# A new order for VectorE's and ScalarE's instructions up to the first FFN tiles

## The chip, the cores and the metric

The kernel runs on one core of one Trainium2 chip, as one launch. The metric is the device time of that launch in microseconds (us), as the median of several runs. A core has five engines that run at the same time, each through its own list of instructions in a fixed order: TensorE (PE, matrix products), VectorE (DVE), ScalarE (ACT), GpSimd (POOL) and SyncE (SP, which here only starts transfers). An engine whose next instruction needs something that is not ready stands still, with all that is behind it in its list. Products land in PSUM, a small memory in eight banks; everything else lies in SBUF.

## The reference, cut to what matters

One layer of a streaming encoder: an SSD (Mamba-2) branch and a latent attention (MLA) branch side by side, then a gated feed-forward network (FFN). There are 512 new tokens of one stream and 64 of another, which has a past.

```python
h = rmsnorm(x, p['norm_mix']);  proj = h @ p['w_in']          # z, xbc, dt, cq, ckv
xbc, conv_new = causal_conv(xbc, conv_buf, p['conv_w'], p['conv_b'])   # 4 taps, then silu
dt = softplus(dt_raw + p['dt_bias']);  A = -exp(p['a_log'])
y, h_new = ssd_scan(xh, dt, A, Bm, Cm, ssm_h0)                # chunked state space scan
y = (y + p['d_skip'][:, None] * xh) * silu(z);  y_ssd = rmsnorm(y, p['ssd_norm'])
q = rmsnorm(cq, p['q_norm']) @ p['w_uq']                      # q_nope, q_rope
q_rope = apply_rope(q[..., QK_NOPE:], cos, sin)
c_kv = rmsnorm(ckv_raw[..., :KV_LORA], p['kv_norm']);  k_rope = apply_rope(...)
o_lat = mla_attend(q_lat, q_rope, ...)                        # softmax over past and new keys
x = x + concatenate([y_ssd, o]) @ p['w_out']
hf = rmsnorm(x, p['norm_ffn'])
x = x + (silu(hf @ p['w_gate']) * (hf @ p['w_up'])) @ p['w_down']
```

The width is 1024, the FFN's 2816, with 8 SSD heads and 8 attention heads of 64. Everything is float32.

## The kernel before

All 576 tokens lie in the free dimension, in two halves of 288. Channels lie in the 128 partitions. A float32 product is made of three products of a rounded type: each operand is split into a high part and the rest (`wh` and `wl` of a weight), and high·high, high·rest and rest·high are added up in PSUM. The split of a weight tile of 128x1024 is a cast on ACT and a subtraction on DVE:

```python
112        act.copy(hi, raw)
113        dve.tensor_tensor(lo, raw, hi.bitcast(F32), ALU.subtract)
```

So each weight tile asks for one transfer (L119), 1.05 us of ACT and 1.22 us of DVE before PE can use it. Raw tiles and both parts share a few buffers in turn (`wpool`), so a split can also have to wait until PE has read an older weight.

The stages up to 280 us, with the lines that matter here:

- First projections and norms, up to about 45 us. L309 scales the compressed query `cq` by its norm, L313 the compressed key `ckv`. `sp_a`, `dt` and `dA` (L346 to L356) are the step sizes of the scan, small instructions on 128x40.
- Input tiles with the convolution, about 40 to 86 us. Eight tiles `ps_in` in the order 3, 6, 0, 2, 4, 1, 5, 7, two PSUM buffers in turn. DVE evicts each with three instructions (L382, L383, L384) into `up`; then ACT makes the first tap (L389), DVE three more (L391, `cacc`), ACT the tanh (L393), and DVE L395 and L396 write the result into `xsd` (tiles 0 to 3) or `bc` (4 to 7). PE can begin a tile when the tile two before it has been evicted.
- Rotary queries. PE makes `ps_qr0` and `ps_qr1` from `cqn` (made by L142 on ACT and L146 on DVE from `cq`), in the same two PSUM buffers. DVE multiplies with cosine and sine: L421 twice reads `ps_qr0` into `rrp`, L422 twice reads `ps_qr1` into `qt`, L423 twice combines them. Then the pool of these two PSUM buffers is closed, and new pools take its space: the first z tile `ps_z0` lies where `ps_qr0` was and so waits until both L421 have read that. POOL copies the rotated queries to their place (L601), and after them applies the causal mask to `cumb` (L500), on which the scan's exponentials `E` on ACT wait (L506).
- Gates `z` and the scan, 88 to 150 us. Halves of `ps_z` are evicted by L453 into `zh`, one of two banks each; ACT makes the tanh (L456) and DVE the gate (L457). For each chunk of tokens DVE makes `xdt` (L485), `xw` (L509), `E` times the products (L514), reads the outputs `ps_y` (L532, L539, L540), multiplies with the gate (L567) and carries the state `h` (L554, L555).
- Attention and the output projection, mixed, 120 to 260 us. `ps_q` and `ps_k` are evicted by L607 and L611, scores `sc` get a maximum (L640, DVE), the exponential with its sum (L641, ACT), and a scaling by the reciprocal (L642, L647); transposes and the products with the values follow (L679 to L704). The output projection's halves `ps_o` are added to the residual `x` by L735.
- FFN tiles from about 222 us to the end.

The order in which the engines go through all this is not the order in which the code makes the instructions. After the whole program is written, a table `ISSUE` names, for each engine, the numbers of its instructions in the order in which they are to be issued, and each is tied to the one before:

```python
1303        for a, b in zip(order, order[1:]):
1304            tc.add_manual_dep(made[b], made[a].name, info, reason="issue order")
```

The numbers count an engine's instructions as they were made; a range such as `67-68` stands for all in it. What an instruction waits for is worked out afterwards from the data and the buffers.

## Time and profile before

| | |
|---|---|
| time, median of 3 runs | 641.3 us (641.02 to 641.71) |
| the profiled execution | 639.76 us, span 638.1 us |
| TensorE | busy 627.0 us, 98% of the span, 4635 matmuls |
| weight load of TensorE | 598.9 us, 94% |
| VectorE | 543.5 us, 85%, 945 instructions |
| ScalarE | 400.9 us, 63%, 768 instructions |
| GpSimd | 110.4 us, 17% |
| TensorE's granted clock, mean | 0.998 of full speed |
| chain that ended last | TensorE 84%, VectorE 3%, ScalarE 1%, transfers 1% |

A row of the timeline gives the start, the time, the engine, the line of the code, the operation, what it writes and reads, the tile's shape, and a count, if several alike stand in a row; in brackets stands how long the engine was idle just before and what ended that. Instructions of one engine overlap a little, so that one row may begin some hundredths of a microsecond before the end of the last. Names come without their numbers in the profile: `ps_in` is any of the eight input tiles.

### The profile page before, as it was taken

To read this page: it belongs to the slowest core of one execution; us is meant where nothing else is said; L and a number is where in the kernel's file an instruction comes from. 1 tells how busy PE (TensorE), PEld (TensorE's weight loads), DVE (VectorE), ACT (ScalarE), POOL (GpSimd) and SP (SyncE) were. 2 spreads that over 40 slices of the span, in tenths; PEclk is the share of its full clock that TensorE was granted. 3 is DMA by queue.
4 is the path that set the end of the run, shared out by engine and by line. 5 is a ranking of instruction groups with operands and counts; after the bars stand their busy time and mean duration, and the time that the engine had idled before them with its cause. 6 is when DMAs were issued, how large, how long until landed. Compare 5 with 4: busy or idle time off the path is not lost.

```text
span 638.1 us, 12090 instructions
## 1 busy us (share of the span) xinstructions
PE 627.0 (98%) x4635; PEld 598.9 (94%) x4635; DVE 543.5 (85%) x945; ACT 400.9 (63%) x768; POOL 110.4 (17%) x164
## 2 busy tenths in 40 slices
PE   9999999999999999999999999999999999999996
PEld 8899999986787799999999999999999999999995
DVE  6999986899876699999999888988899789986555
ACT  7645436778775567766566676566757665767364
POOL 1322103101010000001300330033103220323323
PEclk9999999999999999999999999999999999999999
DMA  9322366322231133235643986398737892589914
GB/s 320 130 61 71 97 158 159 108 80 60 87 123 61 56 111 102 89 116 183 239 141 101 205 185 153 82 186 194 169 100 156 197 206 100 101 211 258 259 27 148
DMA packets 39593, 89.19 MB, mean 140 GB/s; under 512 B 4570, under 2 KB 14312, under 8 KB 39280
## 3 DMA queue, kind: packets, MB, share of 16 engines
q1 hardware_dynamic: 26416, 63.12, 30.5%
q0 software_dynamic: 12400, 24.73, 20.9%
q8 instruction: 36, 0.59, 0.4%
q10 hardware_dynamic: 720, 0.57, 0.3%
q14 instruction: 21, 0.17, 0.1%
HBM read 62.74 MB, written 24.53 MB: 137 GB/s over the span
## 4 chain that ended last, share of the span: by engine, by line
PE 84%; DVE 3%; ACT 1%; issue 1%; POOL 1%; DMA 1%; POOLq 0%; DVEq 0%; ACTq 0%
PE ps_x L852 21%; PE ps_d L1050 14%; PE ps_z L852 11%; PE ps_o L443 8%; PE ps_y L852 5%; PE ps_in L128 4%; PE ps_z L443 3%; PE ps_l L988 3%; PE ps_d L988 2%; PE ps_p L852 2%; PE sc L657 2%; PE pv L704 2%; PE ptp L679 1%; PE ps_v L590 1%; PE ps_q L443 1%
## 5 line engine op out<-in xcount | busy, mean ns | idle before, releaser
L852 PE MATMUL ps_x<-xop,wh_gu_S 128*128 128x288 f32 x504 | 101.7, 295 | 0.0
L852 PEld LDWEIGHTS ps_x<-xop,wh_gu_S 128*128 128x128 f32 x504 | 80.7, 188 | 0.2
L852 PE MATMUL ps_x<-xop,wl_gu_S 128*128 128x288 f32 x252 | 74.0, 294 | 0.0
L113 DVE TENSOR_TENSOR wl_gu_S<-gu,wh_gu_S 128x1024 fp32r<-128x1024 f32 x44 | 53.4, 1221 | 10.3 <-ACT wh_gu_S L112 6.8
L1064 POOL DMA_DIRECT2D acc<-fz x32 | 27.9, 907 | 167.2 <-ACT fz L1061 138.3
L112 ACT CAST wh_gu_S<-gu 128x1024 fp32r<-128x1024 f32 x44 | 46.3, 1052 | 15.9 <-PE ps_y L852 8.2
L852 PEld LDWEIGHTS ps_x<-xop,wl_gu_S 128*128 128x128 f32 x252 | 47.3, 188 | 0.0
L128 PE MATMUL ps_in<-xs,wh_in 128*128 128x288 f32 x256 | 45.3, 298 | 0.8 <-DVE sp_a L351 0.6
L128 PEld LDWEIGHTS ps_in<-xs,wh_in 128*128 128x128 f32 x256 | 37.6, 189 | 1.9 <-issue 0.9
L852 PE MATMUL ps_z<-xop,gu_a 128*128 128x288 f32 x252 | 38.3, 295 | 0.0
L852 PEld LDWEIGHTS ps_z<-xop,gu_a 128*128 128x128 f32 x252 | 35.0, 188 | 0.0
L852 PE MATMUL ps_z<-xop,wh_gu_S 128*128 128x288 f32 x168 | 34.9, 297 | 0.0
L852 PE MATMUL ps_x<-xop,wh_gu_A 128*128 128x288 f32 x168 | 34.6, 297 | 0.0
L852 PE MATMUL ps_y<-xop,wh_gu_A 128*128 128x288 f32 x168 | 33.9, 294 | 0.0
L112 ACT CAST wh_gu_A<-gu 128x1024 fp32r<-128x1024 f32 x22 | 23.1, 1051 | 10.4 <-PE ps_x L852 7.0
L443 PE MATMUL ps_o<-cat_y,wh_out 128*128 128x288 f32 x128 | 29.3, 312 | 0.4 <-ACT cat_y L142 0.4
L113 DVE TENSOR_TENSOR wl_gu_A<-gu,wh_gu_A 128x1024 fp32r<-128x1024 f32 x22 | 26.8, 1220 | 1.4 <-ACT wh_gu_A L112 1.0
L852 PEld LDWEIGHTS ps_z<-xop,wh_gu_S 128*128 128x128 f32 x168 | 27.2, 189 | 0.3 <-ACT wh_gu_S L112 0.3
L128 PE MATMUL ps_in<-xs,wl_in 128*128 128x288 f32 x128 | 27.4, 296 | 0.0
L852 PEld LDWEIGHTS ps_x<-xop,wh_gu_A 128*128 128x128 f32 x168 | 27.2, 189 | 0.1
L852 PEld LDWEIGHTS ps_y<-xop,wh_gu_A 128*128 128x128 f32 x168 | 26.9, 188 | 0.0
L443 PE MATMUL ps_z<-xs,wh_z 128*128 128x288 f32 x128 | 26.4, 299 | 0.0
(384 smaller groups left out, 2012.0 us busy)
## 6 DMA issues: line engine op xcount, KB each, us to landing
gu<-in_w_gu SPq DMA_DIRECT2D x44, 512.0 KB, 5.3
wr_d<-in_w_down SPq DMA_DIRECT2D x18, 512.0 KB, 4.1
acc<-fz POOLq DMA_DIRECT2D x16, 288.0 KB, 6.6
acc<-da POOLq DMA_DIRECT2D x16, 288.0 KB, 7.8
acc<-dc POOLq DMA_DIRECT2D x16, 288.0 KB, 8.4
wr_in<-in_w_in SPq DMA_DIRECT2D x8, 512.0 KB, 3.8
wr_out<-in_w_out SPq DMA_DIRECT2D x8, 512.0 KB, 3.2
cumb<-cumD SPq DMA_DIRECT2D x5, 512.0 KB, 4.6
```

The costliest lines, as they stand in the source:

```text
L112: act.copy(hi, raw)
L113: dve.tensor_tensor(lo, raw, hi.bitcast(F32), ALU.subtract)
L128: pe.matmul(ps[:m, hf, :n], w, x[:, hf * n : (hf + 1) * n], start=start and k == 0 and i == 0, stop=stop and k == last and i == 2,)
L443: pe.matmul(ps[:, :n], w, x[:, cols], start=k == 0 and i == 0, stop=k == len(terms) - 1 and i == 2,)
L590: pe.matmul(ps[:n], l, r, start=j == 0, stop=j == 2)
L657: pe.matmul(s[:, :nk], qs[:, j, q0 : q0 + P], ks[:, j, :nk], start=True, stop=True)
L679: pe.transpose(pp[:, k : k + P], prs[p, i][:, j, b * P : b * P + P], ident)
L704: pe.matmul(pv[64 * j : 64 * j + 64, b * P :], V[b][:, h * HD : (h + 1) * HD], pts[p, b, j], start=b == 0, stop=True, skip_group_check=b > 0,)
L852: pe.matmul(ps, p, q, start=not onto and first and kp == kps[0] and j == 0, stop=onto or (last and kp == kps[-1] and j == 2), skip_group_c ...
L988: pe.matmul(ps, w, x[:, cols], start=first and k == 0 and i == 0, stop=last and k == len(terms) - 1 and i == 2,)
L1050: pe.matmul(ps, p, v, start=not onto and n == 0 and j == 0, stop=onto or (n == len(ks) - 1 and j == 2), skip_group_check=onto,)
L1064: pool.dma_start(out, src, accum_op=ALU.add)
```

## The change

Only the two strings of the table for DVE and ACT are other ones, and in them only the part up to the first FFN tiles: DVE's first 450 numbers or so and ACT's first 340 or so. The lists of PE, POOL and SP are the same, and so are all instructions, their sizes and their buffers. A line of the diff reads:

```diff
     "DVE": """
-1 0 2-3 48 4-5 7 6 9 12 8 10-11 13-15 17 16 18-20 23 21-22 49 24 58 25 30 26 85 27-29 31-34 67-68 106 36 69 108 37 105
...
+195 192 184 193-194 197 185-186 196 224 204 179 207-209 198-203 214 205 288 210 222 211 216 212 217 225 218 213 220
...
     "ACT": """
-0-5 8 6-7 10 9 13 11 14 12 15 17-18 16 21 19 24 20 23 40 22 25 44 26-27 51 28-33 48-49 55 34-35 37 36 59 50 41-42
...
+0-6 8 7 9-10 12 11 14 13 15 18 16-17 19 21 20 24 23 22 40 44 25-27 51 28-29 50 30-31 48-49 32-33 55 34-36 41 59 37
```

What this does is seen in the lists of instructions. Here are three places of DVE's list. In the lists tiles bear a number of the program: `up_631` is the eviction of input tile 6, `up_732` of tile 0, `up_1110` of the last, tile 7, and `cacc` goes with them.

The first place, between 45 and 60 us in the profile before: from behind the eviction of tile 6 to that of tile 0. Before:

```order
L350 SCALAR_TENSOR_TENSOR sp_a<-sp_a,sp_q 128x40
L113 TENSOR_TENSOR wl_in_914<-wr_in_911,wh_in_913 128x1024
L313 TENSOR_TENSOR ckv<-ckf,ckv 128x832
L350 SCALAR_TENSOR_TENSOR sp_a<-sp_a,sp_q 128x40 x3
L391 SCALAR_TENSOR_TENSOR cacc_639<-up_631,hcw,cacc_639 128x579
L350 SCALAR_TENSOR_TENSOR sp_a<-sp_a,sp_q 128x40
L391 SCALAR_TENSOR_TENSOR cacc_639<-up_631,hcw,cacc_639 128x579 x2
L382 TENSOR_TENSOR up_732<-ps_in_683,R_99 128x288
```

And now, where the scaling of `cq`, which stood ahead of tile 6's eviction (between two L391 of tile 3), is the last row:

```order
L350 SCALAR_TENSOR_TENSOR sp_a<-sp_a,sp_q 128x40
L351 SCALAR_TENSOR_TENSOR sp_a<-sp_a,sp_s 128x40
L353 SCALAR_TENSOR_TENSOR dt<-sp_a,dt 128x40
L396 SCALAR_TENSOR_TENSOR xsd<-cth_572,cacc_567 128x64
L313 TENSOR_TENSOR ckv<-ckf,ckv 128x832
L391 SCALAR_TENSOR_TENSOR cacc_639<-up_631,hcw,cacc_639 128x579 x3
L382 TENSOR_TENSOR up_732<-ps_in_683,R_99 128x288
L383 TENSOR_TENSOR up_732<-ps_in_683,R_99 128x224
L384 TENSOR_TENSOR up_732<-ps_in_683,R_99 128x64
L309 TENSOR_TENSOR cq<-cq,Rq 128x1152
```

The scaling of `cq` went behind two evictions, and the subtraction for the weights of tile 1 (`wl_in_914`) behind two as well, to after that of tile 2. Later, the two L146 that make `cqn` from `cq` went from behind the evictions of tiles 2 and 4 to behind those of tiles 1 and 5, and the subtraction for the query weights (`wl_uqr`) from inside the eviction of tile 1 to behind that of tile 5. The subtraction for tile 7's weights stays between the evictions of tiles 4 and 1, but the buffer it now writes is one that the products of tile 1 read.

The second place, 85 to 95 us: from the last row of tile 7's eviction to the second L422. `wl_z_1183` is the rest of the first z tile's weights, `wl_z_1324` of the second's. Before:

```order
L384 TENSOR_TENSOR up_1110<-ps_in_1061,R_99 128x64
L421 TENSOR_TENSOR rrp<-ps_qr_1133,cos_sin 128x576 x2
L395 SCALAR_TENSOR_TENSOR xsd<-cth_979,cacc_974 128x512
L113 TENSOR_TENSOR wl_z_1324<-wr_z_1321,wh_z_1323 128x1024
L391 SCALAR_TENSOR_TENSOR cacc_1118<-up_1110,hcw,cacc_1118 128x579 x2
L396 SCALAR_TENSOR_TENSOR bc<-cth_1051,cacc_1046 128x64
L362 TENSOR_SCALAR ncum<-ps_cum 128x40
L422 TENSOR_TENSOR qt_419<-ps_qr_1146,cos_sin 128x576
L391 SCALAR_TENSOR_TENSOR cacc_1118<-up_1110,hcw,cacc_1118 128x579
L422 TENSOR_TENSOR qt_420<-ps_qr_1146,cos_sin 128x576
```

And now:

```order
L384 TENSOR_TENSOR up_1110<-ps_in_1061,R_99 128x64
L113 TENSOR_TENSOR wl_z_1183<-wr_z_1180,wh_z_1182 128x1024
L391 SCALAR_TENSOR_TENSOR cacc_1118<-up_1110,hcw,cacc_1118 128x579 x2
L421 TENSOR_TENSOR rrp<-ps_qr_1133,cos_sin 128x576 x2
L422 TENSOR_TENSOR qt_419<-ps_qr_1146,cos_sin 128x576
L422 TENSOR_TENSOR qt_420<-ps_qr_1146,cos_sin 128x576
```

A subtraction and two convolution taps came ahead of L421, and L422 follows L421 with nothing between. The subtraction `wl_z_1183` stood two evictions earlier.

The third place, 107 to 113 us: the rows up to the eviction of `ps_z_1_1417`, one half of the third z tile. Before:

```order
L457 SCALAR_TENSOR_TENSOR sz<-zt_1187,zh_1186 128x576
L514 TENSOR_TENSOR E_1266<-E_1266,ps_b_1256 64x4x64 x2
L453 SCALAR_TENSOR_TENSOR zh_1389<-ps_z_1_1417,R_99 128x288
L113 TENSOR_TENSOR wl_uv<-wr_uv,wh_uv 128x512
L532 SCALAR_TENSOR_TENSOR xsd<-xsd,par,ps_y_1280 128x64
```

And now:

```order
L514 TENSOR_TENSOR E_1266<-E_1266,ps_b_1256 64x4x64
L113 TENSOR_TENSOR wl_uv<-wr_uv,wh_uv 128x512
L457 SCALAR_TENSOR_TENSOR sz<-zt_1187,zh_1186 128x576
L457 SCALAR_TENSOR_TENSOR sz<-zt_1328,zh_1327 128x576
L554 TENSOR_TENSOR h_1448<-h_s_1178,el_1244 128x512
L532 SCALAR_TENSOR_TENSOR xsd<-xsd,par,ps_y_1280 128x64 x3
L453 SCALAR_TENSOR_TENSOR zh_1389<-ps_z_1_1417,R_99 128x288
```

The eviction went behind the subtraction for `w_uv`, two gates, the scaling of a state and three reads of `ps_y`.

In the attention part, a scaling by L647 of one softmax tile (128x512) that stood at 190.97 us comes ahead of the residual add L735 that stood at 181.91, and other rows of DVE and ACT there change places by a few. ACT's list has the same instructions up to 280 us in another order as well, its casts of weights mostly by one or two places; its loads of function tables keep theirs.

## The prediction

> **What bounds the kernel now.** I read the page's busy times first, then the idle time of TensorE (PE) by releaser, then a table by stage, then PE and VectorE (DVE) beside each other where PE waits.

> ```profile
> PE 627.0 (98%) x4635; PEld 598.9 (94%) x4635; DVE 543.5 (85%) x945; ACT 400.9 (63%) x768; POOL 110.4 (17%) x164
> ```
> ```profile
> PE sc L657 <- ACT pr L641: 1.1, 2, 0.9
> ```
> ```profile
> 120.00:147.00 27.00, 27.00 (x205) 22.99 (x205) 24.94 (x49) 20.84 (x50) 1.09 (x1) 1.00 0.21 65
> 147.00:166.00 19.00, 17.12 (x91) 11.79 (x90) 18.55 (x43) 15.99 (x45) 1.95 (x4) 1.00 0.37 123
> 166.00:222.00 56.00, 55.97 (x407) 44.39 (x406) 38.00 (x97) 36.55 (x102) 1.91 (x4) 1.00 0.18 63
> 222.00:280.00 58.00, 58.00 (x430) 57.01 (x430) 56.37 (x103) 39.34 (x63) 0.00 (x0) 1.00 0.30 100
> ```

> The columns of the last view are the stretch, its length, then busy time of PE, its weight load, DVE, ScalarE (ACT) and POOL, each with its count of instructions, then the granted clock. PE is busy 98% of the span and its order is not touched, so the change can only fill or open gaps in PE. In the moved part (up to 280 us) these are few: PE lacks 1.88 us of 19 in 147–166, where its largest wait (the first row, for the softmax exponentials L641) lies, 0.03 in 166–222 and nothing from there to 280; the other waits are the four shown below, at 51, 59, 88 and 95. So a shift of PE at 222 us reaches the end whole. What can be won is these gaps, some 4 us; what can be lost is whatever DVE's new order makes PE wait.

> **Convolution, 45 to 60 us: a gain.** PE and DVE where an input tile's PSUM buffer is read out late:

> ```profile
> 51.24 0.43 PE L128 MATMUL ps_in<-xs,wl_in 128*128 128x288 f32 x2
> 51.89 0.78 PE L128 MATMUL ps_in<-xs,wh_in 128*128 128x288 f32 x4 [0.22 <-DVE sp_a L350]
> ...
> 58.08 0.43 PE L128 MATMUL ps_in<-xs,wl_in 128*128 128x288 f32 x2
> 59.14 0.76 PE L128 MATMUL ps_in<-xs,wh_in 128*128 128x288 f32 x4 [0.63 <-DVE sp_a L351]
> ```
> ```profile
> 48.01 1.35 DVE L309 TENSOR_TENSOR cq<-cq,Rq 128x1152 f32<-128x1152 f32 x1
> ...
> 52.62 1.23 DVE L113 TENSOR_TENSOR wl_in<-wr_in,wh_in 128x1024 fp32r<-128x1024 f32 x1 [0.77 <-ACT wh_in L112]
> ...
> 58.78 0.21 DVE L384 TENSOR_TENSOR up<-ps_in,R 128x64 f32<-128x64 f32 x1
> ```

> Two matmuls take 0.27 us from start to start (58.00 us for 430 of them in the stage from 222 on, where PE never waits), so the groups after 51.24 and 58.08 should have begun at 51.51 and 58.35: they are 0.38 and 0.79 late, 1.17 together. Each waits for the last eviction (L384) of a tile two before it. The new order takes the 1.35 us of L309 from ahead of the first eviction and the weight split at 52.62 (1.23, of which the next instruction overlaps 0.08) from ahead of the second as well. Both evictions then come more than 0.8 us sooner, and both gaps close: **−1.17**. The moved rows cost nothing as long as nobody wants them soon: the split belongs to a tile that PE begins at about 66, and cq feeds the query projection near 85.

> **Rotary part, 84 to 96 us: a loss and a gain.** DVE first, then PE:

> ```profile
> 64.85 0.81 DVE L146 SCALAR_TENSOR_TENSOR cqn<-cq,par,cqn 128x576 fp32r<-128x576 f32 x1
> ...
> 75.91 0.22 DVE L384 TENSOR_TENSOR up<-ps_in,R 128x64 f32<-128x64 f32 x1
> ...
> 79.62 0.68 DVE L395 SCALAR_TENSOR_TENSOR bc<-cth,cacc 128x512 f32<-128x512 f32 x1
> ...
> 85.29 0.46 DVE L382 TENSOR_TENSOR up<-ps_in,R 128x288 f32<-128x288 f32 x1 [0.20 <-PE ps_in L128]
> 86.89 1.42 DVE L421 TENSOR_TENSOR rrp<-ps_qr,cos_sin 128x576 f32<-128x576 f32 x2 [0.71 <-PE ps_qr L128]
> 90.31 1.22 DVE L113 TENSOR_TENSOR wl_z<-wr_z,wh_z 128x1024 fp32r<-128x1024 f32 x1 [1.40 <-ACT wh_z L112]
> 91.46 1.67 DVE L391 SCALAR_TENSOR_TENSOR cacc<-up,hcw,cacc 128x579 f32<-128x579 f32 x2
> ...
> 94.69 0.74 DVE L422 TENSOR_TENSOR qt<-ps_qr,cos_sin 128x576 f32<-128x576 f32 x1
> 95.66 1.42 DVE L423 TENSOR_TENSOR rrp<-rrp,qt 128x576 f32<-128x576 f32 x2
> ```
> ```profile
> 88.02 0.43 PE L128 MATMUL ps_qr<-cqn,wl_uqr 128*128 128x288 f32 x2
> 88.46 0.50 PE L443 MATMUL ps_z<-xs,wh_z 128*128 128x288 f32 x2
> ...
> 94.49 0.29 PE L443 MATMUL ps_z<-xs,wh_z 128*128 128x288 f32 x1
> 95.58 0.27 PE L483 MATMUL ps_x<-ident,xsd 128*64 128x128 f32 x1 [0.80 <-DVE qt L422]
> ```

> The first z tile takes the PSUM space that L421 reads: L421 ends at 88.31 and PE goes on at 88.46, 0.15 later. In the new order the split of z's weights (1.15 from 90.31 to 91.46) and two L391 (1.67 less 0.08) stand between the last input tile's eviction and L421. That eviction began at 85.29 and takes 0.9. If DVE is on time for it, 1.17 earlier, L421 ends at 85.29 − 1.17 + 0.9 + 1.15 + 1.59 + 1.42 = 89.2.

> DVE may not be on time. The split of the last input tile's weights now waits for an older weight buffer, so that the eviction two tiles earlier (its L384 ended at 76.13) comes no sooner than before; and both L146, two L395 and the query weights' split, half the size of z's, now stand behind it. From 76.1 on: L395 0.6, L146 0.73, L391 three times 0.82, the next eviction 0.85, L146 0.73, L395 0.6, the split 0.6, L391 three times 0.82, together 9.0. The last eviction begins at 85.1, and L421 ends at 90.1.

> PE resumes at 89.35 or 90.25, where it could have at 88.29 − 1.17 = 87.1: 2.2 to 3.1 of waiting (in the second case some 0.6 of it already at the second ps_qr, which takes the buffer of the last eviction). Against this, L422 follows at once, in the second case until 91.5, and the wait at 95.58 goes: after 94.49 the next matmul should start at 94.62, so 0.96 is won. At that place PE then stands at 89.35 − 88.46 − 0.96 = −0.07 or at 90.25 − 88.46 − 0.96 = **+0.83**; the gain of 1.17 is used up in both. I take the second, since the wait for the buffer follows from the order; both ends stay in the range.

> [...]

> **Gates, 109 to 118 us: a loss.** ACT, PE, then DVE:

> ```profile
> 109.18 0.62 ACT L112 CAST wh_uv<-wr_uv 128x512 fp32r<-128x512 f32 x1
> ```
> ```profile
> 113.44 0.51 PE L443 MATMUL ps_z<-xs,wh_z 128*128 128x288 f32 x2
> ```
> ```profile
> 100.07 0.68 DVE L554 TENSOR_TENSOR h<-h_s,el 128x512 f32<-128x512 f32 x1
> ...
> 107.08 0.74 DVE L457 SCALAR_TENSOR_TENSOR sz<-zt,zh 128x576 f32<-128x576 f32 x1
> ...
> 110.89 0.46 DVE L453 SCALAR_TENSOR_TENSOR zh<-ps_z,R 128x288 f32<-128x288 f32 x1 [2.42 <-PE ps_z L443]
> 111.27 1.39 DVE L113 TENSOR_TENSOR wl_uv<-wr_uv,wh_uv 128x512 fp32r<-128x512 f32 x1
> 112.58 0.27 DVE L532 SCALAR_TENSOR_TENSOR xsd<-xsd,par,ps_y 128x64 f32<-128x64 f32 x1
> ```

> Before, DVE sat idle 2.42 us and evicted z's half (L453) the moment it was ready, so PE's next z half at 113.44 had its buffer. Now the split of w_uv, two L457, a state scaling (L554) and three L532 stand ahead. The split waits for the cast, which ends at 109.80 and, behind a copy that waits for PE, moves with PE. Then, each less the 0.08 that the next overlaps, 1.31 + 2 × 0.66 + 0.6 + 3 × 0.19 + 0.46 = 4.26 gives 114.06 against 113.44, a wait of **+0.6**. If the cast comes earlier than the old spacing says, it is 0; with 0.15 to hand over and a cast a little late, 0.9.

> **Softmax start, 147 to 166 us.** Here PE waits 1.88 in all for DVE (busy 18.55 of 19) and ACT. A PE that comes 1.43 later waits less, by as much as those two do not wait for PE in turn; DVE is idle 2.06 us in 120–147, so it partly does. Between 0 and −1.43 I take **−0.5**. Moved rows of the attention part up to 222 us change what stands ahead of PE's reads by half a microsecond either way; with PE lacking 0.03 us in 166–222 only the bad ones count while the good ones have nothing to win: 0 to +0.9, and I take 0 since most have idle DVE ahead of them. FFN rows: nothing, no wait to win, and PE there is fed by splits far ahead.

> Sum: +0.83 + 0.6 − 0.5 = **+0.93 us** to the profiled execution's 639.76 (span 638.1 and 1.7 around it), which lies 1.5 under the median. On the median of 641.3: **642.2**.

> **The rivals.** A difference under 0.2% (1.28 us: 640.0 to 642.6) is not told from none here.

> *Faster, 639.4.* L423, behind L422, now ends near 93.6 instead of 97.0; the copies of the rotated queries and the mask on POOL follow it, and behind the mask ACT's exponentials:

> ```profile
> 101.30 0.35 ACT L506 ACTIVATE E<-cumb,ncum 64x64 f32<-64x64 f32 x1 [3.51 <-POOL cumb L500]
> ```

> They would start some 3.5 us sooner, and ACT and DVE come to 147 us with less behind them. If that takes all 1.88 there, with the two losses above at their lower ends (−0.07 and 0), it is 641.3 − 1.88 − 0.07 = 639.4. For it speaks ACT's idle 3.51; against it that DVE is busy 24.94 of 27 us from 120 on with PE never waiting. It decides if PE's gaps in 147–166 fall under about 0.6 us.

> *Slower, 643.2.* In attention a scaling of one softmax tile (0.48) is put ahead of the residual add L735 whose PSUM buffer the next query matmul takes:

> ```profile
> 179.52 0.89 DVE L640 TENSOR_REDUCE mx<-sc 128x1 f32<-128x128 f32 x2 [0.79 <-PE sc L657]
> ...
> 181.91 0.46 DVE L735 TENSOR_TENSOR x<-ps_o,x 128x288 f32<-128x288 f32 x1
> ...
> 190.97 0.48 DVE L647 TENSOR_SCALAR pr<-pr,sm 128x512 f32<-128x512 f32 x1
> ```
> ```profile
> 182.49 0.54 PE L443 MATMUL ps_q<-cqn,wh_pair 128*128 128x288 f32 x2
> ```

> L735 ends 0.12 before PE starts; 0.4 from that scaling and up to 0.6 from the queue behind it until 186 us give PE a wait of 0.3 to 0.9. At 0.9, with the softmax part giving back 0.4 and not 0.5, it is 643.2; from 0.4 on it carries the forecast over the bound below. Against it: DVE idles 0.79 just before.

> *Nothing, 641.3.* DVE's and ACT's load before 166 us sets when softmax runs whatever PE did earlier, so all of 1.43 is given back. Then PE's gaps in 147–166 shrink by as much as the waits in 84–118 grow.

> *Clock.* The waits between 85 and 90 could be long enough for the array's clock to drop. The lowest clock of any stretch, at the end where PE has next to nothing to do, gives a price:

> ```profile
> 632.00:638.00 6.00, 0.71 (x7) 0.52 (x5) 2.13 (x6) 0.37 (x1) 1.41 (x2) 0.84 0.54 175
> ```

> 0.16 of 6 us is about 1 us: 643.2. Against it: 1.00 in 147–166 through 1.88 us of gaps. [...]

> **How the numbers follow.** Forecast 0.42 (about 641.5 to 643.2, half of it on each side of 642.6), faster 0.21, slower 0.19, nothing 0.15, clock 0.03. Under 640.0 lie the faster rival and a little of the rest: 0.23. Above 642.6 lie half the forecast, the slower rival and the clock: 0.41. Between: 0.36. The range reaches to the faster rival, 639.4, and up to all losses at their upper ends with nothing given back, 641.3 + 0.83 + 0.9 + 0.9 = 643.9, each with the spread of the three runs before around their median, 0.3 below and 0.4 above.

> **What would show it.** Right: no wait of PE on L350/L351 near 51 and 58; waits of 2 to 3 us in all of ps_qr and ps_z on L384 and L421 between 85 and 90; none of ps_x on L422; a wait of about 0.6 of ps_z on L453 near 114. Wrong: L421 ending before 89, or gaps of PE in 147–166 near zero, would make it faster; PE gaps in 166–222 over 0.5, slower.

## The result, and the profile after

The changed kernel takes 648.67 us (median of 6 runs, 645.73 to 650.11) against 641.16 (6 runs, 640.7 to 641.71): ratio 1.0108, 95% interval 1.0083 to 1.0134. It is slower by 7.5 us, and outside the forecast range. The profiled execution took 649.08 us, with a span of 647.4.

The page of the changed kernel, busy times:

```profile
PE 632.2 (98%) x4635; PEld 602.9 (93%) x4635; DVE 547.0 (84%) x945; ACT 400.7 (62%) x768; POOL 115.6 (18%) x164
```

PE's busy time grew by 5.2 us although its matmuls are the same, so some of them ran longer. PE's idle time by releaser:

```profile
PE ps_z L443 <- DVE rrp L421: 2.2, 1, 2.2
PE sc L657 <- ACT pr L641: 1.1, 2, 0.8
...
PE ps_o L443 <- DVE x L735: 0.7, 1, 0.7
PE ps_z L443 <- DVE zh L453: 0.7, 1, 0.7
PE ps_in L128 <- DVE up L384: 0.7, 1, 0.7
...
PE ps_qr L128 <- DVE up L384: 0.4, 1, 0.4
```

The waits on L421, L453 and the second ps_qr are the forecast ones. Those on L384 for ps_in and on L735 for ps_o were not forecast. The timeline around L421, DVE and then PE:

```profile
86.62 0.45 DVE L382 TENSOR_TENSOR up<-ps_in,R 128x288 f32<-128x288 f32 x1
...
87.42 1.21 DVE L113 TENSOR_TENSOR wl_z<-wr_z,wh_z 128x1024 fp32r<-128x1024 f32 x1
88.55 1.67 DVE L391 SCALAR_TENSOR_TENSOR cacc<-up,hcw,cacc 128x579 f32<-128x579 f32 x2
90.14 1.42 DVE L421 TENSOR_TENSOR rrp<-ps_qr,cos_sin 128x576 f32<-128x576 f32 x2
91.47 0.75 DVE L422 TENSOR_TENSOR qt<-ps_qr,cos_sin 128x576 f32<-128x576 f32 x1
```
```profile
91.70 0.78 PE L443 MATMUL ps_z<-xs,wh_z 128*128 128x288 f32 x2 [2.25 <-DVE rrp L421]
92.27 0.44 PE L443 MATMUL ps_z<-xs,wl_z 128*128 128x288 f32 x1
...
99.40 0.27 PE L483 MATMUL ps_x<-ident,xsd 128*64 128x128 f32 x1
```

The rows stand on each other as forecast, with L421 ending at 91.56 and no wait left at ps_x. But behind the wait a single z matmul takes 0.44 us where it took 0.29 before. The table by stretch shows why (columns as in the prediction, the granted clock third from the right):

```profile
89.00:91.50 2.50, 0.45 (x4) 0.22 (x2) 2.46 (x5) 0.00 (x0) 0.41 (x1) 1.00 1.02 226
92.00:95.00 3.00, 3.00 (x14) 3.00 (x14) 3.00 (x6) 0.55 (x1) 1.03 (x3) 0.50 1.05 257
95.50:98.50 3.00, 3.00 (x25) 3.00 (x24) 1.76 (x4) 0.69 (x2) 3.00 (x6) 1.00 1.11 226
...
163.50:170.00 6.50, 6.07 (x18) 4.29 (x19) 5.34 (x12) 4.73 (x14) 0.85 (x2) 0.50 0.76 269
```

In 92–95, 14 matmuls fill 3 us; in 95.5–98.5, 25 do. The array ran at half clock (granted 0.50) for 3.41 us from 91.75, behind the wait for L421, and again for 6.83 us from 163.43, at the softmax start. In the profile of before the granted clock is 1.00 up to 636.10 us.

Since both kernels issue the same matmuls in the same order, the shift of PE can be read at any of them: the start of the matmul in one trace less the start of the same matmul in the other. Against the profile of before, in us (`a2_again` is a second profile of the changed kernel; the last two are experiments below):

| matmul, at (before) | forecast | changed | a2_again | e3_one_ahead | e4_wout_back |
|---|---|---|---|---|---|
| 85.6, query tile | −1.17 | +0.37 | +0.46 | +0.30 | +0.30 |
| 95.7, ps_x | +0.83 | +3.83 | +2.39 | +0.63 | +0.31 |
| 119.4, z halves done | +1.43 | +5.16 | +3.73 | +1.55 | +1.25 |
| 169.7, softmax start done | +0.93 | +7.68 | +5.27 | +2.04 | +1.73 |
| 227.3, attention | +0.93 | +8.64 | +6.24 | +3.00 | +3.11 |
| 228.6, behind the wait on L735 | +0.93 | +9.62 | +7.14 | +4.09 | +3.11 |
| last | +0.93 | +9.30 | +7.13 | +4.26 | +2.84 |

### The profile page after: what moved, and what is told of

It reads as the page before. It is cut to its first block, busy times and chain, and to the rows that moved or that the text cites. A ratio compares the mean times of both kernels' runs of the same rounds, so it can differ in the third digit from the quotient of the medians.

```text
span 647.4 us, 12087 instructions
## 1 busy us (share of the span) xinstructions
PE 632.2 (98%) x4635; PEld 602.9 (93%) x4635; DVE 547.0 (84%) x945; ACT 400.7 (62%) x768; POOL 115.6 (18%) x164
## 4 chain that ended last, share of the span: by engine, by line
PE 74%; DVE 16%; ACT 4%; issue 3%; DMA 2%; POOL 1%; POOLq 0%; SPq 0%; DVEq 0%; ACTq 0%
PE ps_x L852 20%; PE ps_d L1050 14%; PE ps_z L852 10%; PE ps_y L852 5%; PE ps_z L443 3%; PE ps_first L128 3%; PE ps_l L988 3%; PE ps_in L128 3%; PE ps_o L443 3%; PE ps_d L988 2%; PE sc L657 2%; PE ptp L679 1%; DVE cacc L391 1%; DVE xop L800 1%; PE pv L704 1%
## 5 line engine op out<-in xcount | busy, mean ns | idle before, releaser
L113 DVE TENSOR_TENSOR wl_gu_S<-gu,wh_gu_S 128x1024 fp32r<-128x1024 f32 x44 | 53.3, 1221 | 9.8 <-ACT wh_gu_S L112 6.9
L112 ACT CAST wh_gu_S<-gu 128x1024 fp32r<-128x1024 f32 x44 | 46.3, 1052 | 15.5 <-PE ps_y L852 8.2
L128 PE MATMUL ps_in<-xs,wh_in 128*128 128x288 f32 x256 | 45.3, 298 | 1.1 <-DVE up L384 0.7
L128 PEld LDWEIGHTS ps_in<-xs,wh_in 128*128 128x128 f32 x256 | 37.6, 189 | 2.1 <-PE ps_in L128 0.9
L443 PE MATMUL ps_z<-xs,wh_z 128*128 128x288 f32 x128 | 27.9, 311 | 3.1 <-DVE rrp L421 2.2
L443 PE MATMUL ps_o<-cat_y,wh_out 128*128 128x288 f32 x128 | 29.8, 316 | 0.7 <-DVE x L735 0.7
L112 ACT CAST wh_gu_A<-gu 128x1024 fp32r<-128x1024 f32 x22 | 23.1, 1050 | 11.1 <-PE ps_x L852 7.0
L113 DVE TENSOR_TENSOR wl_gu_A<-gu,wh_gu_A 128x1024 fp32r<-128x1024 f32 x22 | 26.8, 1219 | 1.4 <-ACT wh_gu_A L112 1.0
L128 PE MATMUL ps_in<-xs,wl_in 128*128 128x288 f32 x128 | 27.4, 296 | 0.0
```

The source lines that it names most:

```text
L128: pe.matmul(ps[:m, hf, :n], w, x[:, hf * n : (hf + 1) * n], start=start and k == 0 and i == 0, stop=stop and k == last and i == 2,)
L443: pe.matmul(ps[:, :n], w, x[:, cols], start=k == 0 and i == 0, stop=k == len(terms) - 1 and i == 2,)
```

## The experiments

Medians are compared with runs of the kernel before on the same chip; the ratio has its 95% interval. The numbers in the diffs are the table's: 142 is the last input tile's L384, 149 and 152 are the two L421, 150 and 153 the two L422, 143 to 145 that tile's L391, 155 and 170 the subtractions for the first and the second z tile, 377 the one for `wl_out_0_2789`.

**Which part of the order?** Five kernels take the order of before and of the change in turn along the list. The lists hold the same numbers up to each cut (about 97, 121 and 202 us).

```diff
 h2_new_first   DVE: new[:156] + old[156:]              ACT: new[:78] + old[78:]
 h1_old_first   DVE: old[:156] + new[156:]              ACT: old[:78] + new[78:]
 g1_gates       DVE: old + new[156:188] + old           ACT: old + new[78:119] + old
 g2_softmax     DVE: old + new[188:341] + old           ACT: old + new[119:249] + old
 g3_out_ffn     DVE: old[:341] + new[341:]              ACT: old[:249] + new[249:]
```

> The new order up to about 97 us, the old one behind it. Theory A: wait of 2.2 us on L421 and 3.4 us of half clock as in the changed kernel, PE at +3.8 us at the first ps_x; the old gates add nothing and the softmax start gives back up to 1 us: 644 to 645. Theory C: nearly the whole loss, 647 to 648.7, because the softmax start then falls to half clock as well.

> The old order of VectorE and ScalarE up to about 97 us (156 and 78 numbers), the new one behind it. Theory A: no half clock near 92, PE level with the kernel before at the first ps_x; what the later part does by itself remains: about +1.3 us at the gates, +0.4 in attention, +0.9 at the output projection, 643.8, and about 2 to 3 us more in the executions in which the softmax start near 155 to 165 us still falls to half clock. Theory C (the later part is harmless by itself, and was only hurt by coming 4 to 5 us late): 641 to 642.

> The kernel before with the new order only from 97 to about 121 us (numbers 156 to 188 of VectorE's list, 78 to 119 of ScalarE's). Theory A (each stretch loses by its own waits): a wait of ps_z on L453 of about 0.7 us near 113, or of ps_y on L514 near 110 since the mask now comes no earlier, together +0.9 to +1.3: 642.0 to 642.4. Theory D (the softmax start gives it back): 641 to 641.5.

> The kernel before with the new order only from 121 to about 202 us (188 to 341 of VectorE, 119 to 249 of ScalarE). Theory A: new waits of PE on the sum of squares L569 and on the exponentials L641 at the softmax start, +0.8, and on L607 in attention, +0.4 to +0.8: 642.4 to 642.9, more in executions with half clock there. Theory E (the new order is no worse there, and the 2.5 us lost there in the changed kernel come from half clock alone): 641 to 641.3, with half clock in as many executions as before.

> The kernel before with the new order only from about 202 us on. Theory A (the split of wl_out1_0, moved behind a residual add, holds up a transfer and with it the two FFN weight transfers behind it in SyncE's queue, so VectorE waits for them at L809 and PE for L735): +0.9 us at 227, and +0.3 at 267: 642.2. Rival: without the earlier lateness the transfers come in time: 641.0 to 641.3.

Measured: h2 643.61 (1.0034, 1.002 to 1.0047), h1 644.53 (1.0052, 1.0039 to 1.0065), g1 641.8 (1.0006, 0.9994 to 1.0019), g2 642.51 (1.0023, 1.0011 to 1.0036), g3 642.0 (1.0012, 0.9999 to 1.0026). No part holds the loss alone: the three late parts cost 0.06, 0.23 and 0.12% (the first and the last are by themselves not told from none), 0.41 of h1's 0.52, and h1 and h2 add to 0.86% of the 1.08%. In g3 the largest new wait is one of 1.0 us on L735, at 227 us.

**The place of L421.** It goes back directly behind the last eviction (e1), or behind the weight split but ahead of the taps (e3), in the changed kernel:

```diff
 changed        ... 140-142 155 143-144 149 152 150 153 138 ...
 e1_rope_back   ... 140-142 149 152 155 143-144 150 153 138 ...
 e3_one_ahead   ... 140-142 155 149 152 143-144 150 153 138 ...
```

> The changed kernel with one thing put back: both L421 directly behind the eviction of the last input tile, ahead of z's weight split and the two L391. Theory A (PE's wait of 2.25 us on L421 also brings the array to half clock): the wait and the half clock behind it both go, PE stands at about +0.4 us against the kernel before at the first ps_x instead of +3.8, and the time falls by about 3.4 us from 648.7, to 645. Theory B (the low clock is not due to this wait): the clock still drops somewhere between 85 and 97 us, and only the wait is won, 1.9 us, 646.8. Either way the later losses (gates, softmax, residual adds) stay.

> The changed kernel with both L421 ahead of the two L391 (but still behind the weight split). L421 ends 1.59 us sooner, so the wait of the first z tile falls from 2.25 to about 0.7. If the loss there is the wait alone, the kernel gains 1.6 us on the changed one (about 647). If the wait's length brings the half clock, that goes too: 1.5 more, 645.5, and about as much more again if later stretches at half clock get rarer, 644.5.

e1 took 643.51 (1.0042, 1.0027 to 1.0057), e3 643.64 (1.004, 1.0025 to 1.0055). Two rows in another place return some 5 us of the 7.5. e3's PE:

```profile
90.04 0.50 PE L443 MATMUL ps_z<-xs,wh_z 128*128 128x288 f32 x2 [0.63 <-DVE rrp L421]
```

The wait is 1.6 us shorter than the changed kernel's 2.25, but the median is 5.4 lower than that of the changed kernel on the same chip (`a2_again`, next). So some 3.8 us lie elsewhere: 0.4 in a second wait, at the next z half, which e3 does not have (1.34 against 0.92 from 95.7 to 119.4 in the table), and 3.4 that no wait explains. e3's profile has the full clock everywhere up to 640 us, so the half clock is what remains to explain these.

**Is the half clock there each time?** The changed kernel, unaltered, with a second profile.

> The changed kernel once more, to see whether half clock behind the wait for L421 is there in every execution. If that wait (2.25 us) brings it each time: a row of 0.44 us (two matmuls 0.44 apart) behind it near 92 again, and a median of 648 to 649. If it depends on where the wait falls against a clock window of about 3.4 us that runs by itself: in this profile the lower clock may be missing at 92 and the time is then about 1.5 us lower, with runs spread from 645.5 to 650 as before.

649.07 us (645.82 to 649.72, 1.0107, 1.0086 to 1.0129). The same wait, and this time the full clock behind it:

```profile
91.80 0.50 PE L443 MATMUL ps_z<-xs,wh_z 128*128 128x288 f32 x2 [2.23 <-DVE rrp L421]
92.14 0.29 PE L443 MATMUL ps_z<-xs,wl_z 128*128 128x288 f32 x1
```
```profile
92.00:95.50 3.50, 3.50 (x28) 3.50 (x28) 3.38 (x7) 0.95 (x2) 1.43 (x3) 1.00 1.07 257
...
163.00:166.00 3.00, 3.00 (x7) 1.34 (x6) 3.00 (x8) 1.98 (x4) 0.00 (x0) 0.50 0.88 284
```

The six executions go with their mean granted clock: 645.82 us at 0.999, 646.92 at 0.996 (the profiled one), 648.89 to 649.72 at 0.987 to 0.990. By these six, what the waits alone cost is near 645.8, and the half clock adds an estimated 3 to 4 us in four of them; of the first six executions, one took 645.73 at 0.995.

**Waits of other lengths at the same place**, in the kernel before: rows put between the last eviction and L421.

```diff
 before         ... 140-142 149 152 128 170 143 ...
 d2_wait_1us    ... 140-142 155 128 149 152 170 143 ...
 da_wait_2us    ... 140-142 155 128 137 129 138 104 149 152 170 143 ...
 dc_wait_4us    ... 140-142 170 149 152 128 143 ...
```

> The kernel before with only z's first weight split and one L395 put ahead of L421: PE waits about 1.2 us. Theory A with a threshold near 2 us: no half clock, the mean clock of most executions stays 0.998 to 0.999 as before, and the wait is hidden by the one at 95 us: 641.1. If already 1.2 us is enough in some executions, their clock is 0.994 to 0.997 and the median 641.5 to 642.5.

> The kernel before with only this: z's weight split, two L395 and four small instructions of VectorE put between the last input tile's eviction and L421, so that PE waits about 2.1 us for L421 and nothing else is moved. Theory A (a wait of about 2 us is enough for half clock): PE resumes at 90.3 instead of 88.5, runs at half clock for 3.4 us, and stands at +2.5 us at the first ps_x: 643.7 if in every execution, less in the mean if only in some. [...]

> The kernel before with only the second z weight split, which itself waits for a transfer until 90.3, put ahead of L421. PE then waits about 4.6 us for L421, until 93. Theory A: the clock is at half for at least 3.4 us behind it in every execution, PE stands at +5.2 us at the first ps_x, 646.1. Theory B (no half clock): 644.5.

The waits became 0.94, 1.92 and 4.96 us; the times 640.58 (0.9988, 0.9978 to 0.9999), 641.91 (1.0019, 1.0008 to 1.0029) and 646.02 (1.007, 1.0057 to 1.0084). PE of the three, in that order, with the stretch behind the longest:

```profile
90.59 0.51 PE L443 MATMUL ps_z<-xs,wh_z 128*128 128x288 f32 x2 [0.94 <-DVE rrp L421]
```
```profile
90.61 0.51 PE L443 MATMUL ps_z<-xs,wh_z 128*128 128x288 f32 x2 [1.92 <-DVE rrp L421]
```
```profile
94.17 0.82 PE L443 MATMUL ps_z<-xs,wh_z 128*128 128x288 f32 x2 [4.96 <-DVE rrp L421]
```
```profile
92.00:98.00 6.00, 3.83 (x16) 3.86 (x17) 5.96 (x11) 0.33 (x2) 0.00 (x0) 0.50 1.09 252
```

Behind the wait of 1.92 the granted clock stayed at 1.00 up to 635.4 us in its profile (640.80 us); behind the one of 4.96 it was 0.50 from 91.58 to 98.40, two stretches of 3.41 us. The twelve executions with the wait of 1.92 go from 640.58 us at a mean granted clock of 0.997 to 643.48 at 0.992, so in others of them the clock was lower.

**Four rows back.** e1, with the first eviction ahead of a split (94) and of L403 (109), two z evictions earlier, and split 377 back.

```diff
 e1_rope_back   ... 94 39-41 109 50-52 79 ...    ... 371-372 369 377 373 ...
 e2_four_back   ... 39-41 50-52 109 94 79 ...    ... 377 370-372 369 373 ...
 (and 176, 175 of the z halves, L453, each earlier by some rows)
```

> The changed kernel with four places of VectorE's list put back and nothing else: L421 behind the last eviction; the first input tile's eviction ahead of a weight split (wl_in of tile 2) and one L403; the two evictions of the third z tile as in the kernel before; the split of the first residual weights (wl_out1_0) ahead of two copies L681 instead of behind a residual add. Theory A (the loss is the sum of these waits and of the half clock): against 643.5 with only the first put back, 0.8 at the first eviction, 1.3 at the gates and 0.9 at the output projection come back, 640.5, so no slower than the kernel before. Theory D (the waits only move on to the softmax start, whose own order stays the new one): 642 to 642.5.

648.25 (1.0108, 1.0094 to 1.0121): 7.1 us above the runs of before beside it, where e1 was 2.6 above those beside it, so 4.5 us worse than e1, where it was to be better. PE, ACT and DVE of e2, and ACT of e1:

```profile
55.15 0.76 PE L128 MATMUL ps_in<-xs,wh_in 128*128 128x288 f32 x4 [3.15 <-DVE sp_a L350]
```
```profile
49.02 1.05 ACT L112 CAST wh_in<-wr_in 128x1024 fp32r<-128x1024 f32 x1 [7.50 <-DMA wr_in<-in_w_in]
```
```profile
50.10 1.23 DVE L113 TENSOR_TENSOR wl_in<-wr_in,wh_in 128x1024 fp32r<-128x1024 f32 x1 [2.18 <-ACT wh_in L112]
...
51.67 2.54 DVE L391 SCALAR_TENSOR_TENSOR cacc<-up,hcw,cacc 128x579 f32<-128x579 f32 x3 [0.25 <-ACT cacc L389]
54.13 0.45 DVE L382 TENSOR_TENSOR up<-ps_in,R 128x288 f32<-128x288 f32 x1
```
```profile
46.51 1.05 ACT L112 CAST wh_in<-wr_in 128x1024 fp32r<-128x1024 f32 x1 [4.90 <-DMA wr_in<-in_w_in]
```

Split 94 went from 41.11 to 44.90. A later tile's raw weights land 2.5 us later (the cast at 49.02 instead of 46.51, both waiting for the transfer), and that tile's split, which stands ahead of the taps and the eviction in DVE's list, holds them all. What the transfer itself waits for, in e1 and then in e2:

```profile
SPq L119 <- DVE wl_in L113: 11.3, 1, 11.3
```
```profile
SPq L119 <- PE ps_in L128: 17.3, 1, 17.3
```

In e1 SP starts it at 42.35, right behind split 94, which ends at 42.32. In e2 it starts at 45.37, while split 94 still runs (to 46.11): it now waits for products of PE. A split is not only work for DVE: its place also changes what a later transfer has to wait for. The 3.15 us were not followed by half clock. Nor did the earlier z evictions win anything: the wait of 0.68 on L453 is gone, but PE waits 0.81 for ACT's L506 at 113 us and 0.22 and 0.63 more by 131, and stands 2.77 later than in e1 at the matmul of 147 us. What this and the first wait leave of the 4.5 goes with the clock: e2's four executions have 0.988 to 0.993, e1's nine a median of 0.997.

**The wait at 227 us.** The split 377 alone, on e1.

```diff
 e1_rope_back   ... 368 370-372 369 377 373 ...
 e4_wout_back   ... 368 377 370-372 369 373 ...
```

> The changed kernel with L421 directly behind the last eviction (as in the run that put it back) and with the first output weight's split (number 377) back ahead of the residual add. If that split holds up the transfer queue and through it L809 and the add L735 at 227 us, the wait of 0.8 there goes and the time is 0.8 to 0.9 below the run with L421 put back (about 642.7). If the wait at 227 comes from DVE's load in general, no difference, 643.5.

643.11 (1.0032, 1.002 to 1.0043): 1.75 us above the runs of before beside it, where e1 was 2.62 above those beside it, so 0.9 less (0.6 by the ratios, whose intervals overlap, so the times alone do not decide it). The traces do: in the table the step of 0.9 to 1.1 between 227.3 and 228.6 is 0.00 in e4; 0.4 of it returned at 218 us. In the changed kernel, DVE and SP there:

```profile
228.13 1.22 DVE L113 TENSOR_TENSOR wl_out<-wr_out,wh_out 128x1024 fp32r<-128x1024 f32 x1
231.71 0.46 DVE L735 TENSOR_TENSOR x<-ps_o,x 128x288 f32<-128x288 f32 x1 [2.37 <-PE ps_o L443]
...
234.92 0.69 DVE L809 TENSOR_TENSOR gu<-gu 128x512 f32<-128x512 f32 x1 [1.15 <-DMA gu<-in_w_gu]
235.53 1.22 DVE L113 TENSOR_TENSOR wl_out<-wr_out,wh_out 128x1024 fp32r<-128x1024 f32 x1
236.67 0.45 DVE L735 TENSOR_TENSOR x<-ps_o,x 128x288 f32<-128x288 f32 x1
```
```profile
229.42 0.33 SPq L119 DMA_DIRECT2D wr_out<-in_w_out  x1
229.80 0.42 SPq L806 DMA_DIRECT2D gu<-in_w_gu  x1
```

The split ends at 229.35, and only then SP starts the next `wr_out` and, behind it in its queue, two FFN transfers. L809 waits 1.15 us for the first, with L735 behind it. In e4 both FFN transfers start before 226 us.

**Are the forecast gains to be had?** In the kernel before: the forecast gains of both places (f1), the same without L309 (f2), L422 alone (b1, run twice), and L422 with the last tile's taps earlier too (b2). Here 43 is L309, 121 the subtraction `wl_in_914`, 88 tile 0's L384; f1 also moves ACT's two L142 behind tile 0's L389.

```diff
 before   ... 53 43 54 ... 76 121 45 ... 88 81 ...        ... 149 152 128 170 143-144 138 104 150 145 153 147 ...
 f1       ... 53 54 ... 76 45 ... 88 43 121 81 ...        ... 149 152 150 153 128 170 143-144 138 104 145 147 ...
 f2       ... 53 43 54 ... 76 45 ... 88 121 81 ...        ... 149 152 150 153 128 170 143-144 138 104 145 147 ...
 b1                                                       ... 149 152 150 153 128 170 143-144 138 104 145 147 ...
 b2                                                       ... 149 152 150 153 128 143-145 170 138 104 147 ...
```

> The kernel before with only what the prediction counted as gains: L309 and the weight split of tile 1 behind the eviction of tile 0 (ScalarE's L142, which reads cq, behind the L389 of tile 0), and both L422 directly behind L421. Theory A: the waits at 51, 59 and 95 us go, 0.38 + 0.79 + 0.96, and carry to the end: 638.8. Theory D (what PE wins ahead of 147 us it waits for at the softmax start): PE's waits in 147 to 166 grow from 1.9 to 3 or 4 us, and the time is 640 to 640.9.

> The kernel before with two moves of VectorE's only: both L422 directly behind L421, and the weight split of tile 1 behind the eviction of tile 0. Theory A: 0.8 at 59 us and 0.96 at 95 us are won and reach the end: 639.4. Theory D (what is won ahead of 147 us is waited for at the softmax start): 640.3 to 641.

> The kernel before with one thing of the new order: both L422 directly behind the L421. The prediction prices it at -0.96 (the wait at 95.58 goes). If the rows pushed back by 1.4 us (a split, two L391, L396) are wanted by nobody soon: 640.2. If they return as other waits, as with the gains in the convolution: 641 to 641.5.

> The kernel before with L422 behind L421, once more on another chip or day: at 0.998 with an interval to 0.9992 the gain is as small as the measurement can tell. A real gain of 0.96 less what came back gives 0.998 to 0.9995 again; if the first run was luck, 1.000 to 1.001.

> The kernel before with both L422 directly behind the L421, and the last tile's three taps (L391) ahead of the z weights' split. In the run with L422 alone a wait of 0.6 for bc (L396) and a shift of 0.5 at the next z tile took the place of the 0.96 won. If the taps are what bc waits for, both go: 0.5 to 1.0 us below that run, 639.6 to 640. If the split, now 0.8 later, is wanted at once, no gain on it: 640.4 or more.

f1 took 642.25 (1.0011, 0.9998 to 1.0023), f2 641.14 (0.9996, 0.9985 to 1.0007), b1 640.41 (0.998, 0.9968 to 0.9992) and again 640.11 (0.998, 0.9966 to 0.9993), b2 640.85 (0.9995, 0.998 to 1.001). b1 is ahead of the kernel before by 0.2% in both runs, at the limit of what is told here (d2, with a longer wait, has 0.9988 with an interval that also ends under 1). The traces do not show that gain: PE wins 0.96 at ps_x in both profiles, and by 102 us gives back 1.17 in the first and 0.75 in the second, at ps_b and at the next z half. b1's executions have a mean granted clock under 0.997 in 3 of 12 and 2 of 12, those of before beside them in 16 of 27 and 11 of 22; that its gain is rarer half clock was not tried. The second profile (ps_x started at 95.58 before):

```profile
94.63 0.27 PE L483 MATMUL ps_x<-ident,xsd 128*64 128x128 f32 x1
...
97.41 0.50 PE L443 MATMUL ps_z<-xs,wh_z 128*128 128x288 f32 x2 [0.32 <-DVE zh L453]
```

b2, meant to remove what came back, gained nothing more: 0.84 of the 0.96 is back by 102 us. f1 removed the wait at 51, as forecast, but not the one at 59, which is 1.83. PE, ACT and DVE of f1:

```profile
59.88 0.76 PE L128 MATMUL ps_in<-xs,wh_in 128*128 128x288 f32 x4 [1.83 <-ACT up L381]
```
```profile
52.29 1.05 ACT L112 CAST wh_in<-wr_in 128x1024 fp32r<-128x1024 f32 x1 [5.07 <-DMA wr_in<-in_w_in]
53.35 1.28 ACT L393 ACT_TABLE_LOAD   x1
...
55.50 0.87 ACT L389 ACTIVATE cacc<-up,hcw 128x579 f32<-128x579 f32 x1
```
```profile
56.41 0.82 DVE L391 SCALAR_TENSOR_TENSOR cacc<-up,hcw,cacc 128x579 f32<-128x579 f32 x1 [4.21 <-ACT cacc L389]
...
58.86 0.45 DVE L382 TENSOR_TENSOR up<-ps_in,R 128x288 f32<-128x288 f32 x1
```

DVE, free of the split, waited 4.21 us for ACT. The chain runs from a weight transfer through ACT's cast, its table load and L389 to DVE's taps and the eviction, and in before the split only filled a hole in it: there too L391 waited for L389, the last 0.30 us of it. That wait of PE is not a fixed number either. In the eleven profiles with the order of before up to here it is 0.63 (the profile that the prediction read) to 1.60 us, and where it is long, ACT's cast waits long for the transfer (0.70 us before, 1.64 in d2, where PE waits 1.56). With 1.37, f2 lies inside this spread. f1's tile starts at 59.88, where those of the eleven start at 59.14 to 60.35, so what PE won at 51 it only waited for here.

## Why the prediction was wrong

**Convolution, forecast −1.17, measured +0.37 (+0.46 in the second profile).** This step failed by 1.6 us against the profile that it was read from. That profile is the quickest here: from 45 to 85.6 us the eleven profiles with the order of before take 0 to 0.93 more (median 0.50), the six with the new order −0.04 to +0.30 (median 0.24). So the new order wins some 0.3 by the medians, and 0.9 of the 1.17 did not come. The first tile's eviction, left out of the step altogether, begins 1.68 us later, and the gap at 51 did not close, since DVE's taps now wait for ACT's L389. DVE before, then in the changed kernel:

```profile
35.83 0.74 DVE L154 TENSOR_TENSOR ssq<-ssq,sq 128x576 f32<-128x576 f32 x1
...
43.38 0.45 DVE L382 TENSOR_TENSOR up<-ps_in,R 128x288 f32<-128x288 f32 x1
```
```profile
31.38 1.71 DVE L154 TENSOR_TENSOR ssq<-ssq,sq 128x576 f32<-128x576 f32 x1
...
45.06 0.44 DVE L382 TENSOR_TENSOR up<-ps_in,R 128x288 f32<-128x288 f32 x1
...
49.62 2.54 DVE L391 SCALAR_TENSOR_TENSOR cacc<-up,hcw,cacc 128x579 f32<-128x579 f32 x3 [0.65 <-ACT cacc L389]
```

PE lost 0.84 at this eviction and 0.19 at 51. Almost the same rows stand ahead of the eviction in both lists (four L350 of 0.2 have come, one L402 of 0.74 has gone); 0.97 of the 1.68 is one row of the same size, the addition L154, which takes 1.71 us and not 0.74. It now runs beside POOL's L241 (30.91 to 32.49), where before POOL was idle; that this is why was not tried. The gap at 59 did close (59.14 became 59.56, with PE 1.22 late by then: 0.80 won). But f1 shows that taking away the split and L309 does not close it. What the changed kernel has besides is another order on ACT, which the step did not count; that it is the cause was not tried by itself.

**Rotary part, forecast 2.00 from the query tiles to ps_x (from −1.17 to +0.83), measured 1.93 in the second profile and 3.46 in the first.** The waits were 0.4 and 2.25, 2.7 in all within the forecast 2.2 to 3.1, and −0.96 came as forecast. The step's order and durations were right; the first profile's 1.5 more are the half clock.

**Clock, forecast with 0.03.** This is the step that failed most: the sum put half clock at nothing. That a stall of 2.2 to 3.1 us would leave the clock full was the author's estimate, with one row beside it, 1.00 in 147–166 through 1.88 us of gaps; no run shows that such a stall always does. Waits of 2.25, 2.22 and 1.83 us were followed by half clock, and waits of 2.23 and 3.15 were not: the last section has the rows. Bringing the wait down to 0.63 (e3) took 5.4 us off where the wait itself was 1.6.

**Gates, forecast +0.6, measured +1.33 (from 95.7 to 119.4).** The wait on L453 came as forecast, 0.68, and 0.92 in PE's shift. A second of 0.39 at the next z half came on top, which the step did not follow.

**Softmax, forecast −0.5 given back, measured +0.5 in e3 and e4 at full clock, +1.5 with one stretch at half clock, +2.5 with two.** The sign failed twice. A PE that comes late wins nothing here: in dc_wait_4us, 6.63 late at 147 us, with the old order behind and at full clock there, PE's four waits are 0.23, 0.91, 0.21 and 0.39 us, each as before. And the new order is itself worse: g2, which has it only from 121 to 202 us, shows the same steps at L569 and L641 (0.2 to 0.35 each) and the same 1.5 with one stretch at half clock. The faster rival's condition came about and its gain did not: the exponentials of the scan start at 98.55 instead of 101.30, and yet PE's waits at the softmax start are 2.2 us in all in e3, where they were 1.7 before.

**Attention, forecast 0, measured +1.0 from 169.7 to 227.3** (+1.4 in e4). 0.4 of it lies at the slower rival's place, 181 us, though on L607 and not L735. "FFN rows: nothing" failed by 0.9 to 1.1 at 227, as e4 shows: it overlooked that a split moved on DVE also sets when SP may start the next transfer, and with it those behind that one.

At full clock the failed steps add 1.6 (convolution), 0.7 (gates), 1.0 (softmax), 1.0 (attention) and 0.9 (at 227), 5.2 us, to the sum's 0.93: 6.1 over the 639.76 of the profile of before, and the one execution at 0.999 took 645.82. These are shifts against that one profile, so only the 645.82 is a check, and the convolution's 1.6 holds 0.5 by which that profile was quicker there than the median. The half clock adds an estimated 3 to 4 us in most others. Where the list of one engine alone decided (L421 behind known rows), durations from the trace gave the wait to a few tenths; where a second engine or a queue stood in the chain, they did not.

## What to carry to other kernels

Before a gap is booked as a gain, follow the waiting chain through the other engine and the transfer behind it: a row that fills a hole in DVE's list gives nothing when it leaves. Read a gap that waits for a transfer in several profiles, since here it was 0.63 us in one and 1.60 in another. Keep the row that frees PSUM for TensorE as early in the list as its data allow, and look at what else a subtraction's place decides, above all what the next transfer then waits for. In this kernel, with TensorE busy 98% of the time, a wait of 2.25 us cost 1.5 us more in one profile than one of 2.23 in the next, since the matmuls behind it ran at half clock (0.44 us for one and not 0.29); whether they did changed from one execution to the next.

## What the runs showed of the hardware

| run | wait, us | idle share of the window | the next window |
|---|---|---|---|
| dc_wait_4us | 4.96 | 0.69, 0.76 | half, half |
| changed kernel | 2.25 | 0.66 | half |
| h2_new_first | 2.22 | 0.59 | half |
| f1_two_gains | 1.83 | 0.54 | half |
| e2_four_back | 3.15 | 0.51, 0.41 | full, full |
| a2_again | 2.23 | 0.47, 0.25 | full, full |
| da_wait_2us | 1.92 | 0.17, 0.39 | full, full |
| d2_wait_1us | 1.56, at 59 us | 0.31, 0.15 | full, full |

The wait's length does not order these rows: behind 3.15 us the clock was full, behind 1.83 half. How much of it fell into one window does: in the twenty profiles every window there with a share of 0.54 or more is followed by half clock and none with 0.51 or less. The waits of 3.15, 2.23 and 1.92 us lie across a window's edge, with 0.51 and 0.41, 0.47 and 0.25, 0.17 and 0.39 in the two windows. The grid's place differs from execution to execution: in the two profiles of the changed kernel the half clock at the softmax start begins at 163.43 and 162.62, 0.24 of a window apart. That fits the 4 us by which the runs of one kernel differ. This is read off the traces, not tried by moving the grid.

```profile
55.20:58.20 3.00, 3.00 (x23) 3.00 (x24) 2.93 (x6) 0.80 (x1) 0.12 (x2) 1.00 0.00 0
```
```profile
60.50:63.50 3.00, 3.00 (x16) 3.00 (x15) 3.00 (x6) 2.61 (x4) 1.69 (x2) 0.53 0.03 10
```

```profile
89.28:92.69 3.41, 2.08 (x16) 2.11 (x17) 2.78 (x4) 1.82 (x2) 0.00 (x0) 1.00 1.01 271
```

These are e2 behind its 3.15 us, f1 behind its 1.83, and da_wait_2us: the window that holds 1.33 of its 1.92, with 2.08 of 3.41 us busy (the clock in the next one is 1.00 too).

At the softmax start an idle share of 0.30 to 0.37 was followed by half clock in eleven profiles and a largest share of 0.23 to 0.34 by full clock in nine. Why a smaller share was followed by it there, and not each time, stays open. With the old order there such a stretch costs 0.43 to 0.47 us (five profiles), with the new order 1.0 us more than none, and in three profiles a second stretch followed at once (the changed kernel, e1, e2).
